# A decoder block on one core: k's copy on ScalarE's queue, two places for q and k, reciprocals turned in squares, later fetches

## The chip, the cores and the metric

The kernel runs on one of the eight cores of a Trainium2 chip. The metric is the device time of one execution in microseconds (us); lower is better. A core has five engines that run their own lists of instructions and wait for each other by semaphores: TensorE (PE, matrix products; its weight loads are shown as PEld), VectorE (DVE), ScalarE (ACT), GpSimd (POOL) and SyncE (SP, which here only issues DMA transfers). Transfers are carried out by 16 DMA engines.

## The reference

One layer of a decoder block on x of 512 tokens by 1024 channels, in float32:

```
h = rmsnorm(x);  z = h @ w_in, split into q_r, k_r, v_r, g_r, q_f, k_f, v_f, f_f, a_r, a_f
y_r = W_ro(silu(g_r) * GroupNorm(retention(rot(q_r), rot(k_r), v_r)))      4 heads
y_f = W_fo(attention(norm(q_f), norm(k_f), v_f, log_f))                    8 heads of 64
x = x + W_out(sigmoid(a_r) * y_r + sigmoid(a_f) * y_f)
x = x + W_down(silu(h2 @ W_gate) * (h2 @ W_up)),  h2 = rmsnorm(x)
```

The change lies in the attention of y_f. With c the running sum of log_f, per head:

```
s[q, k] = q.k / 8 + c[q] - c[k]   for k <= q, else -inf
o[q] = sum_k exp(s[q,k] - max) v[k] / sum_k exp(s[q,k] - max)
```

## The kernel before, in words

Channels or tokens lie on the 128 partitions of SBUF. Each matrix product in float32 is made of three products of rounded parts (high and low), written as `three(...)`. Weights come in tiles of 128x1024 (512 KB, raw), are split by ACT (`wh`, line 164) and DVE (`wl`, line 165), and are used by PE. PE's list of instructions is pinned: it runs in the order in which the program names the products (`in_order`, line 65). So does SP's list from line 831 on: `move` (line 71) chains all its transfers, and a transfer that must wait for another holds back all that stand behind it.

The attention runs over 8 heads in four pairs a (heads e = 0 and 1 of a pair lie on the lower and upper 64 partitions), and over four blocks i of 128 queries. The loop at line 914 takes one step s for each (a, e, i), 32 steps, and then some more; n = s % 8 is the step within a pair. In each step stand, in this order:

- `fox_prep` (line 692): scales k (part 0) or q (part 1) of a head. ACT writes the high part to its 64 partitions of tile `tk` or `tq`, DVE writes the low part (for k into `kl`, whose other half is zero). For k, `fox_twice` (line 703) has SP copy the high part to the other 64 partitions by a transfer tk<-tk.
- `fox_scores` (line 713): two products of q with k on PE into one of four PSUM banks; GpSimd adds the mask to the bias `cb`; DVE adds the bias and takes the minimum (line 730); ACT takes the exponential with the row sums (line 732) into `pr`, `rs`.
- `fox_turn` (line 735), two steps later: DVE turns `pr` within squares of 32x32 into `psq` (line 744).
- `fox_put` (line 746): SP stores the squares to DRAM (pd<-psq, 640 KB) and, after the second head of a pair, DVE takes the reciprocals of the row sums `ri` (line 752) and SP stores them turned, as rd<-ri.
- `fox_get` (line 756): SP fetches the squares in turned order (pT<-pd, four transfers of 160 KB) and, for the second head, each reciprocal row spread over 64 partitions (rw<-rd).
- `fox_values` (line 766): 16 products of v with pT, then DVE scales by `rw` (line 776), and ACT and DVE split the result into `ofh`, `ofl`.

Between these, `fill(us)` puts products that do not depend on attention (the projection's last groups, the gates, then the retention branch's output) into PE's list until they fill so many microseconds: `SF` = 0.63, 0.83, 1.57, 1.4 for i = 0 to 3, `VF` = 1.8 ahead of the products with v, `TAIL` = 2.6 in the steps after the last scores. The order of PE's list does not depend on when anything arrives.

For pair a, scores stand at n = 0 to 7. q and k of head 1 are prepared at n = 0 and 1 of the same pair, those of the next pair's head 0 at n = 4 and 5. Squares are put at n = 7 (head 0) and at n = 3 of the next pair (head 1); fetched two steps after that; and the products with v of pair a stand at n = 0 two pairs later. `tk`, `tq` and `kl` have one place for each head of a pair; `pT` has two places.

Of the kernel before, what the change touches and what calls it, by code (L numbers as in the profile page):

```python
# [9 lines left out]
F32 = mybir.dt.float32  # L10
F32R = mybir.dt.float32r
# [3 lines left out]
ALU = mybir.AluOpType  # L15
AX = mybir.AxisListType

P = 128
D = 1024
S = 512  # L20
NT = S // P
NK = D // P
RH, RDK, RDV = 4, 64, 128
FH, FD = 8, 64
# [3 lines left out]
MM3 = 3 / 2400.0  # L28
WARM = 8 * (512,) + 3 * (128,)
NEG = -1e30  # L30
PAD_CST, PAD_FTOK, PAD_SM = 104, 104, 32

C_GMIX = 0
C_GFFN = C_GMIX + NK
# [19 lines left out]
def block_kernel(ctx: ExitStack, tc, x, xT, c_early, c_tab, c_late, w_qf, w_tok, w_vg, w_a, w_y, w_o, w_gu, w_gl, w_dn, w_dh, out):  # L54
    nc = tc.nc
    PS = bass.MemoryType.PSUM
    tt, ts, stt = nc.vector.tensor_tensor, nc.vector.tensor_scalar, nc.vector.scalar_tensor_tensor
# [3 lines left out]
    def after(ins, prev):  # L61

        tc.add_manual_dep(ins.ins, prev.ins.name, mybir.DependencyInfo(mybir.DependencyClass.NoSync, mybir.DependencyReason.DATA), reason="order")
# [7 lines left out]
    def move(to, src):  # L71

        ins = nc.sync.dma_start(out=to, in_=src)  # L73
        if moves[0]:
            if moves[1] is not None:
                after(ins, moves[1])
            moves[1] = ins
        return ins
# [3 lines left out]
    def mm(o, **kw):  # L82
        in_order(nc.tensor.matmul(o, **kw))  # L83
# [4 lines left out]
    def f32(ap):  # L88
        return ap.bitcast(F32)
# [5 lines left out]
    drp = tc.alloc_tile_pool(name="drp", bufs=1, space=bass.MemoryType.DRAM)  # L95
    rwk = tc.alloc_tile_pool(name="rwk", bufs=2, side="left")
    sm = ctx.enter_context(tc.tile_pool(name="sm", bufs=2, side="right"))
# [104 lines left out]
    for k in range(NK):  # L202
# [11 lines left out]
        first = nc.vector.tensor_copy(out=h[:, cs], in_=raw)  # L214
# [7 lines left out]
    for k in range(NK):  # L222
        h, l = first_units[k // 2]
# [29 lines left out]
    nc.gpsimd.memset(ones, 1.0)  # L253
    nc.gpsimd.tensor_scalar_mul(gq, ce[:, C_GQ:C_GQ + 1], FD ** -0.5)
    gk = ce[:, C_GK:C_GK + 1]

    def broadcast_cols(r, dst, wide=None, behind=None):

# [259 lines left out]
    gp = nc.gpsimd  # L518
    ret = [{} for _ in range(NT)]
    fox = {}  # L520
# [137 lines left out]
    def fox_bias(h):  # L658

        cb = fwk.tile([P, S], F32, name="cb", tag="cb", bufs=CBUF)  # L660
        move(cb, cd[h:h + 1, :].broadcast_to([P, S]))
        return cb

    ra, rb = slice(0, FD), slice(FD, P)
# [27 lines left out]
    def fox_prep(a, e, part):  # L692

        r, o = ((ra, rb), (rb, ra))[e]
        z, g = ((kf, gk), (qf, gq))[part]
        zr, gr = z[r, a, :], g[r]
        h = fwk.tile([P, S], F32R, name=("tk", "tq")[part], tag=f"{('tk', 'tq')[part]}{e}", bufs=1)
        act(out=h[r], in_=zr, func=AF.Copy, scale=gr)
        to = h[o] if part else kls[e][r]
        stt(out=to, in0=zr, scalar=gr, in1=f32(h)[r], op0=ALU.mult, op1=ALU.subtract)  # L700
        fox[("k", "q")[part], e] = h

    def fox_twice(e):

        r, o = ((ra, rb), (rb, ra))[e]
        move(f32(fox["k", e])[o], f32(fox["k", e])[r])

    def next_bank():

        fox["banks"] = fox.get("banks", 0) + 1  # L710
        return bank(("sc", "tp")[fox["banks"] % 2])

    def fox_scores(a, e, i):

        tq, tk, kl = fox["q", e], fox["k", e], kls[e]
        if i == NT - 1:
            fox["cb"] = fox["bias"].pop(0)
            if e == 0:
                fox["rs", a] = sm.tile([P, 2, NT], F32, name="rs", tag="rs", bufs=2)
        cb = fox["cb"]  # L720
        n = (i + 1) * P
        m = max(n, 256)
        qs = slice(i * P, n)
        gp.tensor_tensor(out=cb[:, qs], in0=cb[:, qs], in1=mask, op=ALU.add)
        sc = next_bank()
        mm(sc[:, :m], lhsT=tq[:, qs], rhs=tk[:, :m], start=True, stop=False)
        mm(sc[:, :m], lhsT=tq[:, qs], rhs=kl[:, :m], start=False, stop=True)
        pr = fwk.tile([P, n], F32, name="pr", tag=f"pr{i}", bufs=1)
        nm = sm.tile([P, 1], F32, name="nm", tag="nm", bufs=4)
        nc.vector.tensor_tensor_reduce(out=pr[:, :n], in0=cb[:, :n], in1=sc[:, :n], scale=-1.0, scalar=3e38,  # L730
                                       op0=ALU.add, op1=ALU.min, accum_out=nm)
        fox["last"] = act(out=pr[:, :n], in_=pr[:, :n], func=AF.Exp, scale=-1.0, bias=nm, accum_out=fox["rs", a][:, e, i:i + 1])  # L732
        fox["pr", a, e, i] = pr
# [12 lines left out]
    def fox_put(a, e):  # L746

        pd = fox["pd", e] = drp.tile([4, 32, 4, 320], F32, name="pd", tag=f"pd{e}")
        move(pd.rearrange("g m b x -> (g m) (b x)"), fox["sq", a, e].rearrange("p b c j -> p (b c j)"))
        if e:  # L750
            ri = sm.tile([P, 2, NT], F32, name="ri", tag="ri", bufs=2)
            nc.vector.reciprocal(out=ri, in_=fox["rs", a])
            rd = fox["rd", e] = drp.tile([2, NT, P], F32, name="rd", tag="rd")
            move(rd.rearrange("e i p -> p e i"), ri)

    def fox_get(a, e):

        pT = fox["pT", a, e] = fwk.tile([P, 4, 320], F32, name="pT", tag="pT", bufs=PT)
        for b in range(4):
            move(pT[32 * b:32 * b + 32], fox["pd", e][:, :, b, :].rearrange("g m x -> m g x"))  # L760
        if e:
            rw = fox["rw", a] = fwk.tile([P, S], F32, name="rw", tag="rw", bufs=1)
            for h, rows in enumerate((ra, rb)):
                move(rw[rows], fox["rd", e][h:h + 1].rearrange("o i p -> o (i p)").broadcast_to([FD, S]))

    def fox_values(a):

        av = next_bank()
        o = av.rearrange("p (g i j) -> p g i j", g=4, i=NT)
        for k in range(NT):  # L770
            c = TRI[k] + k
            for e in range(2):
                mm(o[e * FD:(e + 1) * FD, :, k:, :].rearrange("p g i j -> p g (i j)"), lhsT=vf[:, k, (2 * a + e) * FD:(2 * a + e + 1) * FD],
                   rhs=fox["pT", a, e][:, :, 32 * c:32 * (c + NT - k)], start=k == 0, stop=k == NT - 1)
        o = o.rearrange("p g i j -> p i g j")
        first = tt(out=o, in0=o, in1=fox["rw", a].rearrange("p (i g j) -> p i g j", i=NT, g=4), op=ALU.mult)
        after(first, split_raw.last[1])
        if a == 3:
            after(first, y_ret.last)
        h, l = (f[:, a, :].rearrange("p (i g j) -> p i g j", i=NT, g=4) for f in (ofh, ofl))  # L780
        cast = nc.scalar.copy(out=h, in_=o)
        after(cast, split_raw.last[0])
        if a == 3:
            after(cast, sigmoid.last)
        tt(out=l, in0=o, in1=f32(h), op=ALU.subtract)
# [110 lines left out]

    fwk = tc.alloc_tile_pool(name="fwk", bufs=2, side="left")
    ofp = tc.alloc_tile_pool(name="ofp", bufs=1, side="right")
    kls = [fwk.tile([P, S], F32R, name="kl", tag=f"kl{e}", bufs=1) for e in range(2)]
    for e, o in enumerate((rb, ra)):  # L900
        gp.memset(f32(kls[e])[o], 0.0)

    fill(CF[2])
    fox["bias"] = [fox_bias(0)]
    for part in range(2):
        fox_prep(0, 0, part)
    fill(CF[3])
    fox_twice(0)
    fox["bias"].append(fox_bias(1))
    fill(PF)  # L910
    ofh = ofp.tile([P, 4, S], F32R, name="ofh")
    ofl = ofp.tile([P, 4, S], F32R, name="ofl")
    chain = [(a, e, i) for a in range(4) for e in range(2) for i in reversed(range(NT))]
    for s in range(len(chain) + 9):
        a, n = s // 8, s % 8
        if n < 2 and a < 4:
            fox_prep(a, 1, n)
        if n in (4, 5) and a < 3:
            fox_prep(a + 1, 0, n - 4)
        if s < len(chain):  # L920
            fox_scores(*chain[s])
        if n == 1 and a < 4:
            fox_twice(1)
        if n == 5 and a < 3:
            fox_twice(0)
        if n in (1, 5) and 2 * a + n // 4 + 2 < FH:
            fox["bias"].append(fox_bias(2 * a + n // 4 + 2))
        if n == 0 and a > 1:
            fill(VF)
            if a == 2:  # L930
                fill.until(8)
            if a == 5:
                ready.append(split_raw(begun.pop(0)))
            fox_values(a - 2)
        if n == 7 and a < 4 or n == 3 and 0 < a < 5:
            fox_put(*chain[s - 7 + 3][:2])
        if n in (1, 5) and 0 < a < 5:
            fox_get(*chain[s - 9 + 3][:2])
        if LAG <= s < len(chain) + LAG:
            fox_turn(*chain[s - LAG])  # L940
        fill(SF[chain[s][2]] if s < len(chain) else TAIL)
# [336 lines left out]
    for k in range(HALF + 2, NF):  # L1278
        prepare(k)
        if k - HALF - 2 in (0, 2):  # L1280

            half = (k - HALF - 2) // 2
            name = ("xfh", "xfl")[half]
# [3 lines left out]
        if k - HALF - 2 in (0, 4):  # L1287
            half = (k - HALF - 2) // 4
            put_squares(SQUARES[-1], half)
            name = ("xfh", "xfl")[half]  # L1290
# [84 lines left out]
    for g in range(4):  # L1375
        if g < 3:
            ws.append(factors(w_dh[g + 1]))
        o = pf[:, g % 2, HALF + 4 * (g // 2):HALF + 4 * (g // 2) + 4, :]
        rows = [out[m * P:(m + 1) * P, :] for m in (2 * g, 2 * g + 1)]
# [7 lines left out]
        x, y, z = (bank(t)[:, 0:HT] for t in ("sc", "acc", "acc"))  # L1387
# [134 lines left out]
```

## Time and profile before

| what | value |
|---|---|
| median of 3 runs | 713.64 us (712.75 to 715.49) |
| profiled execution, its own time | 712.57 us |
| its span, first to last instruction | 710.8 us |
| mean granted clock of TensorE | 0.988 |
| PE, DVE, ACT, POOL busy | 689.8, 534.4, 352.9, 70.1 us |
| moved by DMA | 98.30 MB, 95887 packets |
| attention's first scores to its last products with v | 187.3 to 300.4 us |

How to read it: the profile is one execution. A line of a timeline gives start, duration, engine, line of the kernel, operation and operands, and in brackets the idle time just before and what ended it. In "tk<-tk" the left name is what is written. A row of waits gives who waited for whom: total, times, longest. A stretch's row gives the busy time of each engine in it, the granted clock of TensorE as a share of full speed, the busy share of the DMA engines, and what they moved in GB/s. A transfer's row gives its size and the microseconds from issue to landing. SPq is SP issuing.

### The profile page before, as it was taken

Reading aid. Unit: us, or ns where it says so; the run is one execution under the profiler, and the core shown is the slowest. Engines: PE = TensorE matmul, PEld = TensorE weight load, DVE = VectorE, ACT = ScalarE, POOL = GpSimd, SP = SyncE. Lnnn points to the kernel's source line nnn. Section 1 sums busy time; section 2 is a strip of 40 time slices with the busy share of each in tenths; the row PEclk is TensorE's granted clock in tenths of the full one; section 3 lists DMA queues with packets and bytes.
Section 4 is the critical chain, followed back from the end, with each engine's and each line's share of the span. In section 5 each row is a group of like instructions: output and inputs, shape, how many; then the busy total and the mean of one; then the engine's idle time right before and its main releaser. Section 6 shows DMA issues by size and latency. Waiting matters only on the chain.

```text
span 710.8 us, 9375 instructions
## 1 busy us (share of the span) xinstructions
PE 689.8 (97%) x3407; PEld 568.8 (80%) x3407; DVE 534.4 (75%) x857; ACT 352.9 (50%) x518; POOL 70.1 (10%) x88
## 2 busy tenths in 40 slices
PE   8999999999987888999999999999999999999998
PEld 5888988888774566788887888888888898888898
DVE  6898488765595662378799898888989889556784
ACT  6767453233462443254557656464656466334251
POOL 0004940200221210000031000000000000000000
PEclk9999999999998998999999999999999999999999
DMA  8900315437478798433921333637271441551221
GB/s 293 414 8 30 120 60 146 114 105 174 154 187 200 171 192 222 148 118 101 325 109 60 134 116 89 200 86 206 48 214 35 119 161 42 142 190 60 72 96 71
DMA packets 95887, 98.30 MB, mean 138 GB/s; under 512 B 67928, under 2 KB 72664, under 8 KB 95328
## 3 DMA queue, kind: packets, MB, share of 16 engines
q1 hardware_dynamic: 95696, 97.67, 46.9%
q8 instruction: 27, 0.44, 0.3%
q14 instruction: 20, 0.16, 0.1%
q10 hardware_dynamic: 144, 0.02, 0.0%
HBM read 81.90 MB, written 9.47 MB: 129 GB/s over the span
## 4 chain that ended last, share of the span: by engine, by line
PE 85%; DMA 9%; DVE 3%; issue 1%; SPq 1%; ACT 1%; DVEq 0%; ACTq 0%
PE acc L83 65%; PE sc L83 14%; PE tp L83 5%; DMA pd<-psq 4%; DMA pT<-pd 3%; DMA raw<-in_w_tok_dram 1%; SPq L73 1%; PE tp L86 1%; DMA raw<-in_w_a_dram 1%; DVE pr L730 0%; DVE wl L165 0%; ACT ps L1042 0%; DVE psq L744 0%; DVE ps L1043 0%; DVE b L1051 0%
## 5 line engine op out<-in xcount | busy, mean ns | idle before, releaser
L83 PE MATMUL acc<-ps,xfh 128*128 128x512 f32 (+1 forms) x576 | 167.7, 373 | 0.4 <-ACT us L1164 0.4
L83 PEld LDWEIGHTS acc<-ps,xfh 128*128 128x128 f32 x576 | 105.1, 188 | 20.3 <-ACT us L1164 0.6
L1042 ACT CAST ps<-b 128x1024 fp32r<-128x1024 f32 (+1 forms) x84 | 82.3, 980 | 60.9 <-PE acc L83 26.2
L1043 DVE TENSOR_TENSOR ps<-b,ps 128x1024 fp32r<-128x1024 f32 (+1 forms) x84 | 94.4, 1135 | 22.2 <-ACT ps L1042 21.0
L83 PE MATMUL acc<-ps,xfl 128*128 128x512 f32 (+1 forms) x288 | 107.5, 373 | 0.0
L164 ACT CAST wh<-raw 128x1024 fp32r<-128x1024 f32 (+1 forms) x44 | 46.1, 1049 | 90.5 <-PE acc L83 42.9
L165 DVE TENSOR_TENSOR wl<-raw,wh 128x1024 fp32r<-128x1024 f32 (+1 forms) x44 | 55.3, 1259 | 17.6 <-ACT wh L164 17.6
L83 PEld LDWEIGHTS acc<-ps,xfl 128*128 128x128 f32 x288 | 54.2, 188 | 10.4 <-DVE xfl L1005 0.5
L83 PE MATMUL acc<-xh,wh 128*128 128x512 f32 x128 | 52.5, 410 | 0.0
L83 PE MATMUL acc<-xh,wl 128*128 128x512 f32 x128 | 51.7, 404 | 0.8 <-DVE wl L165 0.8
L1051 DVE TENSOR_TENSOR b<-b,b 128x1024 f32<-128x1024 f32 (+1 forms) x48 | 52.1, 1126 | 0.0
L83 PE MATMUL acc<-xl,wh 128*128 128x512 f32 x128 | 51.7, 404 | 0.0
L83 PE MATMUL acc<-wh,xh 128*128 128x512 f32 (+2 forms) x144 | 50.7, 352 | 0.0
L83 PE MATMUL acc<-wh,xl 128*128 128x512 f32 (+2 forms) x144 | 49.8, 346 | 0.0
L83 PE MATMUL acc<-wl,xh 128*128 128x512 f32 (+2 forms) x144 | 49.7, 345 | 0.0
L83 PE MATMUL acc<-hl,ps 128*128 128x512 f32 x168 | 40.8, 392 | 0.0
L83 PEld LDWEIGHTS acc<-hl,ps 128*128 128x128 f32 x168 | 31.6, 188 | 7.0
L1164 ACT COPY us<-acc 128x512 f32<-128x512 f32 (+1 forms) x48 | 26.2, 551 | 17.3 <-PE acc L83 16.3
L732 ACT ACTIVATE pr<-pr,nm 128x512 f32<-128x512 f32 (+3 forms) x32 | 18.0, 561 | 25.8 <-DVE nm L730 25.6
L1083 DVE TENSOR_TENSOR ps<-raw,ps 128x1024 fp32r<-128x1024 f32 x14 | 17.1, 1223 | 17.9 <-ACT ps L1080 17.9
L83 PEld LDWEIGHTS acc<-xh,wl 128*128 128x128 f32 x128 | 24.9, 194 | 7.1 <-DVE wl L165 1.2
L83 PEld LDWEIGHTS acc<-wh,xh 128*128 128x128 f32 x144 | 27.1, 188 | 3.9 <-DVE sT L564 0.2
(301 smaller groups left out, 1458.7 us busy)
## 6 DMA issues: line engine op xcount, KB each, us to landing
b<-in_w_gu_dram SPq DMA_DIRECT2D x40, 512.0 KB, 4.8
raw<-in_w_a_dram SPq DMA_DIRECT2D x16, 512.0 KB, 4.5
raw<-in_w_dn_dram SPq DMA_DIRECT2D x14, 512.0 KB, 4.3
pd<-psq SPq DMA_DIRECT2D x8, 640.0 KB, 6.7
pT<-pd SPq DMA_DIRECT2D x32, 160.0 KB, 4.2
pf<-squares SPq DMA_DIRECT2D x160, 32.0 KB, 1.9
blk<-in_w_vg_dram SPq DMA_DIRECT2D x8, 512.0 KB, 7.7
raw<-in_w_tok_dram SPq DMA_DIRECT2D x8, 512.0 KB, 3.5
```

What stands on the lines that cost most here:

```text
L73: ins = nc.sync.dma_start(out=to, in_=src)
L83: in_order(nc.tensor.matmul(o, **kw))
L86: in_order(nc.tensor.transpose(out=o, in_=src, identity=ident))
L164: split_raw.last = (nc.scalar.copy(out=h[:, :width], in_=raw[:, :width]), tt(out=l[:, :width], in0=raw[:, :width], in1=f32(h)[:, :width], ...
L165: tt(out=l[:, :width], in0=raw[:, :width], in1=f32(h)[:, :width], op=ALU.subtract))
L732: fox["last"] = act(out=pr[:, :n], in_=pr[:, :n], func=AF.Exp, scale=-1.0, bias=nm, accum_out=fox["rs", a][:, e, i:i + 1])
L1042: part.cast = nc.scalar.copy(out=h, in_=raw)
L1043: low = tt(out=l, in0=raw, in1=f32(h), op=ALU.subtract)
L1051: queue(tt(out=raws[g][b][v], in0=raws[g][b][v], in1=raws[g][c][v], op=ALU.add))
L1083: tt(out=l, in0=raw, in1=f32(h), op=ALU.subtract)
L1164: copy = nc.scalar.copy(out=u_(tp, slot), in_=os[tp][:, :w])
```

## The change

Five edits in the attention stage, in one diff:

- k's copy to the other 64 partitions is issued from ACT's list, right behind ACT's scaling, instead of from SP's chained list.
- `tk`, `tq` get two places per head, `kl` two sets by the pair's parity. Preparation moves: head 0 of the next pair at n = 2 and 3, head 1 at n = 6 and 7 (the first pair's head 1 stays at steps 0 and 1).
- The 8 columns of reciprocals go into a zeroed tile of 128x32, DVE turns its four squares of 32x32, and 128 rows of 32 numbers are stored; the fetch takes four pieces of 128 numbers for each partition, and `rw`'s order within a row becomes (g, i, j) instead of (i, g, j).
- `fox_get` stands three steps behind `fox_put` instead of two, and `fox_values` one step later, behind the scores of n = 1; the loop has one step more.
- The pad of the pool of small tiles is 16 columns instead of 32.

```diff
-PAD_CST, PAD_FTOK, PAD_SM = 104, 104, 32
+PAD_CST, PAD_FTOK, PAD_SM = 104, 104, 16
...
+    ri = sm.tile([P, 32], F32, name="ri", tag="ri", bufs=1)
+    nc.gpsimd.memset(ri, 0.0)
...
-        h = fwk.tile([P, S], F32R, name=("tk", "tq")[part], tag=f"{('tk', 'tq')[part]}{e}", bufs=1)
+        h = fwk.tile([P, S], F32R, name=("tk", "tq")[part], tag=f"{('tk', 'tq')[part]}{e}", bufs=2)
         act(out=h[r], in_=zr, func=AF.Copy, scale=gr)
-        to = h[o] if part else kls[e][r]
+        if part == 0:
+            nc.scalar.dma_start(out=f32(h)[o], in_=f32(h)[r])
+        to = h[o] if part else kls[a % 2][e][r]
         stt(out=to, in0=zr, scalar=gr, in1=f32(h)[r], op0=ALU.mult, op1=ALU.subtract)
-        fox[("k", "q")[part], e] = h
-
-    def fox_twice(e):
-
-        r, o = ((ra, rb), (rb, ra))[e]
-        move(f32(fox["k", e])[o], f32(fox["k", e])[r])
+        fox[("k", "q")[part], a, e] = h
...
         if e:
-            ri = sm.tile([P, 2, NT], F32, name="ri", tag="ri", bufs=2)
-            nc.vector.reciprocal(out=ri, in_=fox["rs", a])
-            rd = fox["rd", e] = drp.tile([2, NT, P], F32, name="rd", tag="rd")
-            move(rd.rearrange("e i p -> p e i"), ri)
+            nc.vector.reciprocal(out=ri[:, 0:2 * NT], in_=fox["rs", a].rearrange("p e i -> p (e i)"))
+            rt = sm.tile([P, 32], F32, name="rt", tag="rt", bufs=1)
+            nc.vector.transpose(out=rt, in_=ri)
+            rd = fox["rd", e] = drp.tile([P, 32], F32, name="rd", tag="rd")
+            move(rd, rt)
...
             for h, rows in enumerate((ra, rb)):
-                move(rw[rows], fox["rd", e][h:h + 1].rearrange("o i p -> o (i p)").broadcast_to([FD, S]))
+                row = fox["rd", e].rearrange("(g x) j -> x g j", g=4)[4 * h:4 * h + 4].rearrange("i g j -> g i j")
+                row = bass.AP(tensor=row.tensor, offset=row.offset, ap=[[0, FD], [32 * 32, 4], [1, 4 * 32]])
+                move(rw[rows].rearrange("p (g x) -> p g x", g=4), row)
...
-    kls = [fwk.tile([P, S], F32R, name="kl", tag=f"kl{e}", bufs=1) for e in range(2)]
-    for e, o in enumerate((rb, ra)):
-        gp.memset(f32(kls[e])[o], 0.0)
+    kls = [[fwk.tile([P, S], F32R, name="kl", tag=f"kl{b}{e}", bufs=1) for e in range(2)] for b in range(2)]
+    for pair in kls:
+        for e, o in enumerate((rb, ra)):
+            gp.memset(f32(pair[e])[o], 0.0)
...
-    for s in range(len(chain) + 9):
+    for s in range(len(chain) + 10):
         a, n = s // 8, s % 8
-        if n < 2 and a < 4:
-            fox_prep(a, 1, n)
-        if n in (4, 5) and a < 3:
-            fox_prep(a + 1, 0, n - 4)
+        if n % 4 < 2 and s < 4:
+            fox_prep(0, 1, n)
+        if n % 4 in (2, 3) and a < 3:
+            fox_prep(a + 1, n // 4, n % 4 - 2)
...
-        if n == 0 and a > 1:
+        if n == 1 and a > 1:
             fill(VF)
...
-        if n in (1, 5) and 0 < a < 5:
-            fox_get(*chain[s - 9 + 3][:2])
+        if n in (2, 6) and 0 < a < 5:
+            fox_get(*chain[s - 10 + 3][:2])
```

More of the change, by code (lines that the diff above doesn't have):

```diff
@@ L713, in fox_scores @@
     def fox_scores(a, e, i):
-        tq, tk, kl = fox["q", e], fox["k", e], kls[e]
+        tq, tk, kl = fox["q", a, e], fox["k", a, e], kls[a % 2][e]
         if i == NT - 1:
@@ L775, in fox_values @@
         o = o.rearrange("p g i j -> p i g j")
-        first = tt(out=o, in0=o, in1=fox["rw", a].rearrange("p (i g j) -> p i g j", i=NT, g=4), op=ALU.mult)
+        first = tt(out=o, in0=o, in1=fox["rw", a].rearrange("p (g i j) -> p i g j", i=NT, g=4), op=ALU.mult)
         after(first, split_raw.last[1])
@@ L907, in block_kernel @@
     fill(CF[3])
-    fox_twice(0)
     fox["bias"].append(fox_bias(1))
@@ L913, in block_kernel @@
     chain = [(a, e, i) for a in range(4) for e in range(2) for i in reversed(range(NT))]
-    for s in range(len(chain) + 9):
+    for s in range(len(chain) + 10):
         a, n = s // 8, s % 8
-        if n < 2 and a < 4:
-            fox_prep(a, 1, n)
-        if n in (4, 5) and a < 3:
-            fox_prep(a + 1, 0, n - 4)
+        if n % 4 < 2 and s < 4:
+            fox_prep(0, 1, n)
+        if n % 4 in (2, 3) and a < 3:
+            fox_prep(a + 1, n // 4, n % 4 - 2)
         if s < len(chain):
             fox_scores(*chain[s])
[L922 to L927, printed above, removed]
-        if n == 0 and a > 1:
+            if n in (1, 5) and 2 * a + n // 4 + 2 < FH:
+                fox["bias"].append(fox_bias(2 * a + n // 4 + 2))
+        if n == 1 and a > 1:
             fill(VF)
```

## The prediction

> **What bounds the kernel now.** I read the page's busy times first, then the chain of waits of TensorE (PE), then the stretches that those waits name, then the transfers in them.
>
> ```profile
> PE 689.8 (97%) x3407; PEld 568.8 (80%) x3407; DVE 534.4 (75%) x857; ACT 352.9 (50%) x518; POOL 70.1 (10%) x88
> ```
>
> PE is busy for 97% of the span, so an edit that touches no matrix product can win only what PE waits, and what it runs slowly. PE's own waits are nearly all of one place:
>
> ```profile
> PE tp L83 <- DMA tk<-tk: 6.8, 1, 6.8
> PE tp L83 <- DMA pT<-pd: 4.1, 1, 4.1
> PE sc L83 <- DMA tk<-tk: 3.1, 1, 3.1
> ```
>
> Two are for k's copy (tk), one for the turned exponentials (pT); all lie in the attention steps. The stretches, with columns span, PE, PEld, DVE, ACT and POOL busy, granted clock, DMA share, GB/s:
>
> ```profile
> 211.40:218.25 6.85, 0.02 (x1) 0.03 (x1) 5.09 (x14) 2.65 (x8) 0.46 (x1) 0.83 0.83 14
> 218.25:222.70 4.45, 4.45 (x11) 3.48 (x11) 1.36 (x3) 0.81 (x2) 0.87 (x2) 0.50 0.96 218
> 238.75:241.90 3.15, 0.06 (x1) 0.03 (x1) 1.89 (x5) 2.40 (x6) 0.32 (x1) 1.00 0.11 11
> 243.25:246.60 3.35, 3.35 (x8) 1.76 (x7) 2.37 (x7) 0.82 (x2) 0.46 (x1) 0.50 1.07 247
> 264.60:268.70 4.10, 0.00 (x0) 0.02 (x1) 1.26 (x2) 1.04 (x1) 0.00 (x0) 0.80 0.89 229
> 268.70:273.90 5.20, 5.19 (x16) 2.96 (x17) 0.66 (x1) 0.00 (x0) 0.00 (x0) 0.50 0.54 209
> 208.00:218.00 10.00, 3.42 (x17) 2.69 (x16) 8.43 (x22) 4.40 (x11) 1.38 (x3) 0.89 0.68 23
> 235.00:243.00 8.00, 4.91 (x24) 3.79 (x23) 5.90 (x15) 3.97 (x10) 2.31 (x4) 1.00 0.43 43
> 257.00:265.00 8.00, 7.58 (x33) 5.35 (x31) 5.37 (x19) 2.62 (x8) 1.39 (x3) 1.00 0.91 59
> ```
>
> Rows 1, 3 and 5 are the idle stretches; behind each, rows 2, 4 and 6, PE runs at half clock. The last three rows tell why: from 208 to 218 us the DMA engines are busy for 0.68 of the time and move 23 GB/s. Something occupies them and carries nothing. What the queue of SP issued there, and what that stretch's transfers took:
>
> ```profile
> 207.28 0.38 SPq L73 DMA_DIRECT2D rd<-ri  x1
> 207.76 0.54 SPq L73 DMA_DIRECT2D tk<-tk  x1
> 208.39 0.54 SPq L73 DMA_DIRECT2D cb<-cd  x1
> 210.25 3.69 SPq L73 DMA_DIRECT2D pT<-pd  x4
> ```
>
> ```profile
> DMA packets 1250, 0.59 MB, mean 53 GB/s; under 512 B 1072, under 2 KB 1072, under 8 KB 1250
> ...
> tk<-tk SPq DMA_DIRECT2D x1, 128.0 KB, 10.4
> ```
>
> And how long the four transfers of the reciprocals took to land:
>
> ```profile
> DMA to landing us min/median/max: 10.6/11.9/11.9
> ```
>
> The reciprocals, 4 KB, go out as `rd.rearrange("e i p -> p e i")`: 1024 single elements, which are the 1072 small packets. The first takes 10.6 us, and tk, issued 0.5 us later on the same queue, lands 10.4 us after its issue, when PE has stood since 211.4. The other two waits have an rd ahead of them as well (the last two rows of the stretches). So the culprit is the form of a 4 KB transfer, and the waits on tk and pT are its symptoms.
>
> **The change part by part.** First what there is to win, in the profiled execution (712.57 us, span 710.8; the runs' median is 713.64, so 1.07 us above it).
> Idle: 6.85 + 3.15 + 4.10 = 14.1 us.
> Half clock: half of 4.45 + 3.35 + 5.20 = 13.0, so 6.5 us.
> Waits inside the products with v:
>
> ```profile
> 223.02 1.07 PE L83 MATMUL sc<-pT,vf 128*64 128x512 f32 x2
> 224.38 2.34 PE L83 MATMUL sc<-pT,vf 128*64 128x512 f32 x14 [0.29 <-DMA pT<-pd]
> ...
> 245.75 3.64 PE L83 MATMUL tp<-pT,vf 128*64 128x512 f32 x16
> ...
> 298.08 2.38 PE L83 MATMUL sc<-pT,vf 128*64 128x512 f32 x16
> ```
>
> The last 16 products run unhindered in 2.4; the first set takes 3.7 (to 226.72), the second 3.6, of which 0.4 is clock already counted; the third's first two took about 0.8 too long. Together 1.3 + 0.8 + 0.8 = 2.9. In all 23.5 us; it is gone only if all three edits below work.
>
> *The reciprocals in squares.* Gone: 1024 elements of 4 B. New: 128 rows of 128 B, one DVE transpose of 128x32, and a fetch whose rows are four pieces of 512 B in place of one of 2 KB. Prices from the nearest rows:
>
> ```profile
> pd<-psq SPq DMA_DIRECT2D x8, 640.0 KB, 6.7
> pT<-pd SPq DMA_DIRECT2D x32, 160.0 KB, 4.2
> ...
> kf<-zd SPq DMA_DIRECT2D x4, 256.0 KB, 5.6
> ```
>
> kf<-zd writes runs of 128 B, 2048 a transfer, in 5.6 us; a sixteenth of that many cannot take longer, so rd lies between nearly nothing and 5.6; I take 3, nearer the small end. The fetch gets 512 pieces instead of 128 a pair, a quarter of one kf's and four times as long each: inside 5.6 as well, and needed only when the products are done. The transpose is under the 282 ns below, four times, 1.1 us of DVE at most:
>
> ```profile
> L744 DVE STREAM_TRANSPOSE psq<-pr 128x128 f32<-128x128 f32 x16 | 4.5, 282 | 0.0
> ```
>
> *k's copy on ScalarE, two places.* The copy leaves SP's list, where it stood behind rd and behind SP's waits for pd, and is prepared six steps ahead of its first product instead of three to four:
>
> ```profile
> 187.20:211.40 24.20, 24.20 (x115) 20.03 (x113) 21.68 (x59) 15.59 (x37) 7.27 (x14) 1.00 0.67 201
> 199.60:211.40 11.80, 11.80 (x56) 9.69 (x54) 11.07 (x31) 7.47 (x19) 2.73 (x6) 1.00 0.77 216
> 187.20:275.00 87.80, 73.45 (x313) 54.83 (x312) 58.27 (x151) 38.24 (x88) 16.99 (x30) 0.90 0.80 192
> 153.00:172.00 19.00, 19.00 (x92) 15.53 (x91) 11.07 (x32) 4.98 (x6) 1.04 (x2) 1.00 0.61 148
> ```
>
> ```profile
> L73 SPq DMA_DIRECT2D tk<-tk x8: 467/485/692, 176.0 to 245.6; - x8
> ```
>
> Eight steps take 11.8 us, so six give 8.9. A landing behind rd took 10.4; without rd, a fifth of what the four pT move (four at 160 KB against one of 128) should not take longer than pT's 4.2. ACT pays eight issues of about 0.5 us (SP's price), 4 us over the whole stage, and is busy 7.47 of 11.80: hidden. A new wait: the issue waits for the scaled copy just ahead on ACT, and the next exponentials queue behind it; half a microsecond, against three steps (4.4 us) that PE's four score banks allow. The two further memsets go to POOL, whose only work from 153 to 172 us is the old two (1.04): hidden. DVE is close to full, 11.07 of 11.80; the work is the same but moves forward. DVE spent 21.7 + 5.1 us from 187.2 to 218.25 (5.1 is in the first idle stretch) on what PE will now pass in 24.2, so it falls some 2.6 us behind, inside the same 4.4 us. I charge nothing, up to 2.6.
>
> *Fetches a step later.* The products with v move with them. From putting the squares (n = 3) to using them there were five steps and 1.8 us of filling, 9.2 us; now six, 10.7. Needed are the landings of pd and of pT, 6.7 + 4.2 = 10.9, as measured with rd in the way. So this is what is late next: by the medians 0.2 us at each of three places, none if both get faster, and several if the engines are crowded. I take 2.5 us in all, bounds 0 and 14.5 (rival 1). At the end the last products come one step (2.6 us) later, with other filling ahead of them:
>
> ```profile
> 300.39 0.50 PE L83 MATMUL acc<-orh,wh 128*128 128x512 f32 x1
> 308.19 0.39 PE L83 MATMUL acc<-ofh,wh 128*128 128x512 f32 x1
> ```
>
> Between the last products with v and the first use of ofh lie 7.8 us; 5.2 remain, hidden still. The pad of the small tiles moves no work: nothing.
>
> Sum: 712.57 - 23.5 + 2.5 = 691.6; plus the 1.07 between profile and median, 692.6: I say 692.5.
>
> **The rivals.**
> *1. The DMA engines become the bound* (27%). Of the 87.8 us from 187.2 to 275 they were busy 0.80, 70 us. rd's part is 6.8 + 3.4 + 7.3 = 17.5 us in its three stretches, less about 3.7 for the 1.05 MB that moved beside it (at 216 / 0.77 = 280 GB/s): 13.8. So 56 us of transfers must pass in 64 to 66 us, 85 to 88%. Against it: in the first 24.2 us PE ran without a wait at a share of 0.67. If each of two or three fetches comes 3.15 us late and costs half clock as the second wait did (3.35 / 2), that is 4.8 each: 698.7 to 703.6 (two or three), about a microsecond more in the median. The Trainium skill, "DMA: Bandwidth & Descriptors", section "Issuing engines are not separate DMA queues", speaks for this rival: transfers issued from ScalarE run on the same 16 engines as those from SP, and the second issuer saves only sequencer time. By that rule the copy's new queue wins nothing by itself, and the gain hangs on rd alone; no run here shows it yet. On the clock its "TensorE: Matmul & The Clock Gate", section "What's actually happening", lets the clock fall after an idle window of about 3.4 us; by that a 3.15 us wait could be free, and this rival would end near 697 to 699. The row differs: 3.15 us idle was followed by 0.50.
>
> *2. The transfer stays slow* (8%): a landing of rd near 10 us whatever its form, with tk and pT held up as now; then only the extra step helps, 709 to 714. Against it: kf<-zd moves 16 times as many such rows in 5.6.
>
> *3. Slower: ACT stands at its own queue* (5%). If the issue on ACT holds it until the copy gets through, the exponentials behind it come late, then squares, pd and pT. At 10.4 us a copy, less the 4.4 of slack, six copies inside the chain cost 36 us: 712.6 - 23.5 + 36 = 725. It decides from 4.4 + 23.5 / 6 = 8.3 us a copy on. SP's four issues at 210.25 took 3.69, 0.9 each, with the queues at their fullest: far from 8.3.
>
> **How the numbers follow.** Forecast 60%: 690 to 696. Rival 1 27%: 697 to 705. Rival 2 8%, rival 3 5%. The range reaches from 688 (every microsecond of the 23.5 won gives 690.1 in the median; two below that for the waits I did not count) to 704, leaving out the end of rival 1 and the other two. A measurement of this kernel tells 0.5%, 3.6 us, from no change: faster 0.60 + 0.27 + 0.01 of rival 2 = 0.88, same 0.07, slower 0.05.
>
> **What would show it.** Right: rd's landing under 6 us and no stretch with busy DMA engines at 20 to 60 GB/s; PE's waits on tk gone; the granted clock at 1.00 through the steps; the products with v at 2.4 us; what is left of waiting named pT. Wrong: rd still near 10 us (rival 2); waits on pT of 3 us or more at a high DMA share (rival 1); ACT idle behind its own issues and PE waiting for score banks (rival 3); or PE waiting for DVE, which would mean that the 2.6 us are not covered.

## The result, and the profile after

The changed kernel takes 684.48 us (median of four executions), the kernel before 713.32 us on the same chip: a ratio of 0.9585 [0.9557, 0.9613], or 28.8 us. The forecast was 692.5 us with a range of 688 to 704, so the direction is right and the size is not: the time lies 8 us below the forecast and 3.5 us below the lower end. Three of the four took 683.42 to 684.76 us, and the ratio is theirs; the fourth ran at a granted clock of 0.851 throughout (743 us). The profile shown is of the repeat described below (685.45 us, span 683.7).

The head of the page after, with the granted clock in 40 slices:

```profile
span 683.7 us, 9374 instructions
...
PE 676.1 (99%) x3407; PEld 566.4 (83%) x3407; DVE 534.3 (78%) x861; ACT 354.7 (52%) x518; POOL 70.0 (10%) x91
...
PEclk9999999999999999999999999999999999999999
```

The same row of the page before:

```profile
PEclk9999999999998998999999999999999999999999
```

PE's idle time is 683.7 - 676.1 = 7.6 us; before it was 710.8 - 689.8 = 21.0. So 13.4 us of the 27.1 between the two spans come from idle time, and 13.7 from products that are busy for less time. The slices at reduced clock are gone, and that is part of the 13.7. It can't be all: the forecast counted 6.5 us for it, and 2.9 for waits inside the products with v.

PE's waits after (in total, times, longest):

```profile
PE acc L83 <- DVE wl L165: 1.5, 1, 1.5
PE tp L83 <- DVE warm L114: 1.2, 1, 1.2
PE sc L83 <- DVE wh L214: 0.8, 1, 0.8
PE tp L83 <- DMA pT<-pd: 0.4, 1, 0.4
PE acc L83 <- ACT us L1162: 0.3, 1, 0.3
PE sc L83 <- DMA pT<-pd: 0.3, 1, 0.3
```

The two waits for k's copy are gone, and of the 4.4 us for pT (4.1 and 0.3) 0.7 are left, in two places. The transfers of the attention stage after, first by group (KB each, median us to landing), from 184 to 282 us:

```profile
pd<-psq SPq DMA_DIRECT2D x8, 640.0 KB, 5.5
pT<-pd SPq DMA_DIRECT2D x32, 160.0 KB, 4.1
...
tk<-tk ACTq DMA_DIRECT2D x4, 128.0 KB, 4.0
rd<-rt SPq DMA_DIRECT2D x4, 16.0 KB, 4.8
```

The reciprocals land in 4.8 us (median; 4.3 to 7.9) where they took 11.9, k's copy in 4.0 where the one behind them took 10.4. The issues of k's copy on ACT, for all eight:

```profile
L702 ACTq DMA_DIRECT2D tk<-tk x8: 468/476/519, 173.3 to 213.7; - x8
```

And the attention stage by windows, from the first scores to the first use of ofh (span, PE, PEld, DVE, ACT and POOL busy, granted clock, DMA share, GB/s), with its two most crowded stretches below; then the same stage before:

```profile
186.40:284.70 98.30, 97.66 (x459) 76.37 (x458) 68.12 (x167) 50.11 (x103) 15.54 (x30) 1.00 0.73 220
212.00:232.00 20.00, 19.64 (x93) 15.02 (x92) 15.42 (x45) 10.18 (x25) 5.08 (x10) 1.00 0.93 253
232.00:256.00 24.00, 23.72 (x115) 17.16 (x114) 17.70 (x48) 10.16 (x22) 2.77 (x6) 1.00 0.81 261
```

```profile
187.30:308.20 120.90, 106.55 (x460) 80.60 (x459) 71.76 (x167) 52.05 (x107) 16.99 (x30) 0.93 0.75 182
```

The stage went from 120.9 to 98.3 us. Those 22.6 us are a little more than the forecast had for the whole change (23.5 - 2.5 = 21.0). The rest, 27.1 - 22.6 = 4.5 us of span, lies outside the attention, in stages whose instructions the change does not touch. The same 32 products with ofh, before and after (ns min/median/max, first and last start):

```profile
L83 PE MATMUL acc<-ofh,wh x32: 392/395/398, 308.2 to 329.9; 128*128 128x512 f32 x32
```

```profile
L83 PE MATMUL acc<-ofh,wh x32: 389/389/389, 284.7 to 305.8; 128*128 128x512 f32 x32
```

From the first to the last they take 21.7 us before and 21.1 after. Between the first and the last of the 32 lie 31 groups of three, 93 steps: 0.2333 us a product before, 0.2269 after, 2.7% less, without a wait on either side. The duration of one (395 and 389 ns) shows the difference weakly, since products overlap; the spacing is what counts. Products of this shape are in every stage. That is the part of the 28.8 us that the forecast did not have.

### The profile page after: what moved, and what is told of

It is laid out like the page before. It is cut to its first block, busy times and chain, and to the rows that moved or that the text cites. A ratio compares the mean times of both kernels' runs of the same rounds, so it can differ in the third digit from the quotient of the medians.

```text
span 741.4 us, 9374 instructions
## 1 busy us (share of the span) xinstructions
PE 735.5 (99%) x3407; PEld 581.3 (78%) x3407; DVE 538.3 (73%) x861; ACT 354.5 (48%) x518; POOL 70.0 (9%) x91
## 3 DMA queue, kind: packets, MB, share of 16 engines
q10 hardware_dynamic: 784, 1.07, 0.5%
## 4 chain that ended last, share of the span: by engine, by line
PE 73%; DVE 0%; issue 0%
PE acc L83 56%; PE sc L83 12%; PE tp L83 4%; PE tp L86 0%; DVE pf L1407 0%
## 5 line engine op out<-in xcount | busy, mean ns | idle before, releaser
L83 PE MATMUL acc<-ps,xfh 128*128 128x512 f32 (+1 forms) x576 | 180.0, 396 | 0.0
L83 PEld LDWEIGHTS acc<-ps,xfh 128*128 128x128 f32 x576 | 108.1, 194 | 28.3
L83 PE MATMUL acc<-ps,xfl 128*128 128x512 f32 (+1 forms) x288 | 114.1, 396 | 0.0
L83 PEld LDWEIGHTS acc<-ps,xfl 128*128 128x128 f32 x288 | 55.7, 193 | 13.7
L83 PE MATMUL acc<-xh,wl 128*128 128x512 f32 x128 | 53.4, 417 | 1.4 <-DVE wl L165 1.4
L83 PE MATMUL acc<-xl,wh 128*128 128x512 f32 x128 | 53.3, 417 | 0.0
L83 PE MATMUL acc<-wh,xh 128*128 128x512 f32 (+2 forms) x144 | 53.2, 369 | 0.0
L83 PE MATMUL acc<-wh,xl 128*128 128x512 f32 (+2 forms) x144 | 52.1, 362 | 0.0
L83 PE MATMUL acc<-wl,xh 128*128 128x512 f32 (+2 forms) x144 | 52.0, 362 | 0.0
L83 PE MATMUL acc<-hl,ps 128*128 128x512 f32 x168 | 44.4, 417 | 0.0
L83 PEld LDWEIGHTS acc<-wh,xl 128*128 128x128 f32 x144 | 28.0, 194 | 4.7
```

## The experiments

The change has three parts of work, called squares (the reciprocals turned in squares), k's copy (on ScalarE, two places, earlier preparation) and later fetch. It also moves addresses. The tiles at the right-hand end of SBUF are laid down from the top, the small tiles first: before, ri has 2 x 32 bytes a partition and the pad 128, together 192; after, ri 128, rt 128 and the pad 64, together 320. Everything below them starts 128 bytes lower. In the built programs xh starts at byte 194176 of its partition before, which is 128 past a multiple of 256, and at 194048 after, a multiple of 256.

My theory after the result: the squares carry the gain of the attention stage, as forecast, and the start addresses of product operands carry the rest. The rival: the products run faster for another reason that comes with the work (a clock that never falls, quieter transfers), and the pad does nothing. The runs stand in three groups, each on one chip with its own runs of the kernel before (714.04 us for the first four, 714.33 for the next four, 714.86 for the last four). A ratio is always to the kernel before in the same group; a difference of less than a microsecond between groups shows nothing.

**The changed kernel once more.** No edit.

> The changed kernel once more, for an undisturbed profile. Expected 683 to 686 us. The sum had 23.5 us to win and the runs show 28.8. Theory A (the waits were counted too small): PE idle falls by about 15 us and the rest lies between 187 and 300 us of the old span, the stage as a whole being 28 us shorter. Theory B (something outside the stage): the stage is 23 us shorter and about 5 us are missing after it, with equal counts of products.

684.75 us (683.69 to 685.75), ratio 0.9583 [0.9553, 0.9612]. The result stands, and theory B came true: the stage is 22.6 us shorter, and 4.5 us are missing outside it. The profile is the one shown above.

**The squares alone.** The two other parts undone, the pad of the changed kernel left:

```
-        if part == 0:
-            nc.scalar.dma_start(out=f32(h)[o], in_=f32(h)[r])
+    def fox_twice(e):
...
+        move(f32(fox["k", e])[o], f32(fox["k", e])[r])
...
-        if n in (2, 6) and 0 < a < 5:
-            fox_get(*chain[s - 10 + 3][:2])
+        if n in (1, 5) and 0 < a < 5:
+            fox_get(*chain[s - 9 + 3][:2])
```

> Only the reciprocals in squares; k's copy, one place and old fetch steps as before. Theory 1 (rd's 1024 elements hold up everything behind them): 690 to 697 us, rd lands in under 6 us, no stretch with busy DMA engines at under 60 GB/s, tk's waits gone or under 1 us, pT's 0 to 2 us each. Theory 2 (tk's place in SP's list and its short lead are the cause): 707 or more, tk's waits stay.

686.91 us (686.76 to 687.34), ratio 0.9614 [0.9587, 0.9641]: all but 2.2 us of the change, and below the 690 to 697 that were expected, because these addresses are the new ones too (the same part at the old ones is timed below). PE's waits in its profile:

```profile
PE sc L83 <- DMA pT<-pd: 1.3, 1, 1.3
...
PE tp L83 <- DMA pT<-pd: 0.8, 1, 0.8
PE tp L83 <- DMA tk<-tk: 0.2, 1, 0.2
```

k's copy is issued by SP and prepared as late as before, and the wait for it falls from 9.9 us to 0.2 (0.6 at the old addresses). So the wait named tk was indeed a symptom of what stood ahead of tk on the queue.

**k's copy alone.** The squares and the later fetch undone:

```
-            nc.vector.transpose(out=rt, in_=ri)
-            move(rd, rt)
+            move(rd.rearrange("e i p -> p e i"), ri)
...
-        if n in (2, 6) and 0 < a < 5:
+        if n in (1, 5) and 0 < a < 5:
```

> Only k's copy on ScalarE's queue, with the two places and the earlier preparation; rd in single elements and old fetch steps. Theory 1: tk's waits go, but rd still lands after 10 us and pT behind it, so the first products with v wait 6 to 9 us in place of the scores: 702 to 711 us. Theory 2: 693 to 698, with pT's waits no longer than before (4.4 us in all).

712.7 us (711.24 to 716.29), ratio 0.9982 [0.9961, 1.0002]: no change, where theory 1 had expected a gain of 3 us or more. PE's waits, and the landing of k's copy:

```profile
PE tp L83 <- DMA pT<-pd: 8.0, 2, 4.5
PE sc L83 <- DMA pT<-pd: 7.1, 1, 7.1
```

```profile
DMA to landing us min/median/max: 2.2/3.8/10.7
```

The waits for tk are gone and 15.1 us for pT stand in their place (before: 4.1 for pT, 14.0 with tk). One copy still took 10.7 us although it had ScalarE's queue to itself. It was issued at 207.98 us, while the reciprocals, issued at 204.72, were under way, and from 208 to 216 us all transfers together moved 13 to 36 GB/s. So SP's list isn't what slowed it; that it shares the DMA engines with the single elements is the reading that fits, and is not shown apart. Here the Trainium skill, "DMA: Bandwidth & Descriptors", section "Issuing engines are not separate DMA queues", agrees with the trace: it says that another issuer saves only the sequencer's time, and this run gives the ratio 0.9982.

**k's copy and later fetch, without the squares.** Only the squares undone. The pad is 32 here, so that without the tiles of the squares xh starts at 194176 again, as in the kernel before:

```
-            rd = fox["rd", e] = drp.tile([P, 32], F32, name="rd", tag="rd")
-            move(rd, rt)
+            rd = fox["rd", e] = drp.tile([2, NT, P], F32, name="rd", tag="rd")
+            move(rd.rearrange("e i p -> p e i"), ri)
```

> The changed kernel with rd in single elements again (copy on ScalarE, two places, later fetches kept). Theory 1: 700 to 710 us, waits on pT or rw behind rd at three places. Theory 2: 684 to 690, the squares add little.

709.88 us (708.56 to 710.09, and once 1740.37), ratio 0.9931 [0.9897, 0.9966]. PE's waits:

```profile
PE tp L83 <- DMA pT<-pd: 8.3, 2, 8.1
PE sc L83 <- DMA pT<-pd: 3.1, 1, 3.1
```

Against k's copy alone the extra step takes about 4 us off the waits for pT, and no more: the slow transfer of the reciprocals still stands ahead of the fetch (issued at 206.45 us, the fetch at 216.18).

**The addresses alone, on the kernel before.** No part of the change; the pad puts xh at 194048, as after:

```
-PAD_CST, PAD_FTOK, PAD_SM = 104, 104, 32
+PAD_CST, PAD_FTOK, PAD_SM = 104, 104, 64
```

> The kernel before with one number changed: the pad of the small tiles is 64 columns instead of 32, so that xh, xl, orh, ofh and the feed-forward's tiles start 128 bytes lower, at the addresses they have in the changed kernel (multiples of 256 bytes). Theory B1 (PE reads operands at these addresses faster): 707.5 to 709.5 us, products of 128x512 at 389 ns outside the attention steps instead of 392 to 395. Theory A (all of the 28.8 us lies in the attention's waits): 712.5 to 715.

707.58 us (705.95 to 708.56), ratio 0.9906 [0.9875, 0.9936]. The products with ofh, and PE's waits:

```profile
L83 PE MATMUL acc<-ofh,wh x32: 389/389/389, 307.0 to 328.1; 128*128 128x512 f32 x32
```

```profile
PE tp L83 <- DMA tk<-tk: 9.8, 1, 9.8
PE sc L83 <- DMA tk<-tk: 4.6, 1, 4.6
PE tp L83 <- DMA pT<-pd: 3.5, 1, 3.5
```

The same instructions with the same waits become faster by 6.7 us, and the products with ofh take 21.1 us again. The rival is out: no part of the work is in this run. PE's waits for transfers grew, from 14.0 to 17.9 us in these rows: where a transfer sets the pace, faster products arrive earlier and wait.

**The change without the move of addresses.** The pad puts xh at 193920, 128 past a multiple of 256, as before:

```
-PAD_CST, PAD_FTOK, PAD_SM = 104, 104, 16
+PAD_CST, PAD_FTOK, PAD_SM = 104, 104, 48
```

> The changed kernel with a pad of 48 columns: the same tiles start at 128 bytes past a multiple of 256, as in the kernel before. Theory B1: 688.5 to 691, products at 392 to 395 ns. Theory A: 684 to 685.5.

691.38 us (691.27 to 691.6), ratio 0.9687 [0.9653, 0.972]. This is the change as the prediction costed it, without the move of addresses, and it is 1.1 us from its 692.5. The products with ofh, and the attention stage between the same two places as above:

```profile
L83 PE MATMUL acc<-ofh,wh x32: 390/392/404, 287.3 to 308.9; 128*128 128x512 f32 x32
```

```profile
187.20:287.30 100.10, 99.20 (x460) 76.54 (x459) 68.77 (x167) 49.76 (x104) 15.53 (x30) 1.00 0.72 216
```

The spacing is the old one (21.6 us), and the stage takes 100.1 us: 20.8 less than before.

**Two more addresses.** The pad at 32 (xh at 193984, 192 past a multiple of 256) and at 80 (193792, a multiple of 256 that is not one of 512):

```
+PAD_CST, PAD_FTOK, PAD_SM = 104, 104, 32
```

> The changed kernel with a pad of 32 columns: the tiles start at 192 bytes past a multiple of 256 (64 past a multiple of 128). If what counts is a multiple of 256: as slow as with 48 columns or slower, 689 to 693. If only multiples of 128 were good and 256 better: slower than with 48. Theory A: 684 to 685.5.

```
+PAD_CST, PAD_FTOK, PAD_SM = 104, 104, 80
```

> The changed kernel with a pad of 80 columns: the tiles start at a multiple of 256 again, 256 bytes lower (256 past a multiple of 512). If a multiple of 256 is what counts: 684 to 685.5 as the changed kernel. If 512 is needed: 688 or more.

At 192 past: 690.35 us (689.87 to 691.53), ratio 0.9675 [0.9634, 0.9716], the slow time. At a multiple of 256: 684.68 us (683.9 to 684.83), ratio 0.959 [0.9557, 0.9623], the fast time. A multiple of 512 isn't needed.

**The squares alone, at the old addresses.** The second experiment with the pad at 48 (xh at 193920):

```
-PAD_CST, PAD_FTOK, PAD_SM = 104, 104, 16
+PAD_CST, PAD_FTOK, PAD_SM = 104, 104, 48
```

In the next texts e2 is the squares alone at the new addresses, and e6 the change with the pad at 48.

> Only the reciprocals in squares, and a pad of 48 columns, so that the tiles start at 128 past a multiple of 256 as in the kernel before. This is the squares' own part. From e2 (686.9) plus the 6.7 us between e6 and the changed kernel: 692 to 695 us, a ratio near 0.972. If the address counts only together with the other edits: 687 to 689.

694.15 us (693.56 to 695.17), ratio 0.9709 [0.9695, 0.9724]. This one part is worth 20.7 us of the 28.8 by itself, against about 7 for the address and 2 to 3 for all the rest.

**The squares with one of the other two parts each.** First with k's copy (the later fetch undone), then with the later fetch (k's copy undone), both at the new addresses:

```
-        if n in (2, 6) and 0 < a < 5:
-            fox_get(*chain[s - 10 + 3][:2])
+        if n in (1, 5) and 0 < a < 5:
+            fox_get(*chain[s - 9 + 3][:2])
```

> The changed kernel without the later fetches (squares, k's copy on ScalarE and two places, new addresses). Of the 2.2 us between e2 and the changed kernel: if they are tk's and the SP list's relief, 684.5 to 685.5 here; if they are the later fetch's, 686.5 to 687.5, with waits on pT of about 2 us.

```
-            nc.scalar.dma_start(out=f32(h)[o], in_=f32(h)[r])
+        move(f32(fox["k", e])[o], f32(fox["k", e])[r])
```

> The changed kernel without k's copy on ScalarE and its two places (squares, later fetches, new addresses). If the later fetch brings what is left: 684 to 685.5, waits on pT under 1 us; if the copy does: 686.5 to 687.5, with waits on tk or pT.

With k's copy: 690.96 us (689.48 to 691.87), ratio 0.9656 [0.9638, 0.9675]. With the later fetch: 687.97 us (687.6 to 688.85), ratio 0.9623 [0.9609, 0.9637]. Both are slower than everything that was expected. The squares alone have 686.91 us, ratio 0.9614, in another group. By the ratios k's copy makes them about 3 us slower (4 by the medians), the later fetch alone changes nothing clear of the noise, and the two together make them 2.2 us faster. PE's waits with k's copy:

```profile
PE tp L83 <- DMA pT<-pd: 3.3, 2, 2.0
...
PE tp L83 <- DVE nm L729: 0.9, 1, 0.9
...
PE sc L83 <- DVE nm L729: 0.5, 1, 0.5
```

The last two are new: PE waits for a score bank that DVE has not read. But DVE is not short of time. Behind those waits stand these of DVE (200 to 260 us) and of POOL (same stretch):

```profile
DVE pr L729 <- POOL cb L723: 7.8, 7, 3.9
```

```profile
POOL cb L723 <- DMA cb<-cd: 7.1, 2, 4.6
```

And SP's list in that place:

```profile
213.08 0.55 SPq L73 DMA_DIRECT2D raw<-in_w_a_dram  x1
219.18 0.35 SPq L73 DMA_DIRECT2D pd<-psq  x1
219.64 0.39 SPq L73 DMA_DIRECT2D raw<-in_w_a_dram  x1
220.12 0.89 SPq L73 DMA_DIRECT2D cb<-cd  x1
```

SP issues nothing from 213.63 to 219.18, and the table of biases (cb), which POOL, DVE and then PE need, stands behind. In the changed kernel cb is issued at 217.27. So the chain is SP's list, cb, POOL, DVE, PE. The profile puts 5.5 us of SP's wait down to the landing of a copy of k; why the earlier fetch sets it off was not tried apart, nor whether the queue or the earlier preparation costs the 3 to 4 us.

With the later fetch alone, one wait for a transfer is left, and the clock shows what it costs (the products with v around it, then the stretch behind it and a longer one):

```profile
212.75 1.07 PE L83 MATMUL tp<-pT,vf 128*64 128x512 f32 x2
216.77 3.94 PE L83 MATMUL tp<-pT,vf 128*64 128x512 f32 x14 [2.95 <-DMA pT<-pd]
```

```profile
217.00:220.00 3.00, 3.00 (x11) 1.59 (x10) 1.73 (x3) 1.46 (x3) 0.15 (x1) 0.50 0.81 250
212.00:232.00 20.00, 17.05 (x74) 12.29 (x73) 15.87 (x41) 10.47 (x26) 4.36 (x9) 0.91 0.88 247
```

After 2.95 us of idle the 14 products take 3.94 us instead of 2.34, at a granted clock of 0.50. The Trainium skill, "TensorE: Matmul & The Clock Gate", section "What's actually happening", gives an idle window of about 3.4 us before the clock falls; the idle times recorded here (2.95 us, and 3.15 before the change) are shorter. How far they contradict it is open, since the ends of products are modelled in these profiles: the two products ahead of this wait are recorded with 1.07 us, where sixteen unhindered ones take 2.38. The longest wait in the run with k's copy, 2.0 us, cost no clock (granted 1.00).

**The other operand.** The changed kernel, its right-hand tiles at the fast address, with the tiles at the left-hand end of SBUF moved by 128 bytes: wh and wl start 128 past a multiple of 256 (byte 14464 in place of 14336).

```
-PAD_CST, PAD_FTOK, PAD_SM = 104, 104, 16
+PAD_CST, PAD_FTOK, PAD_SM = 136, 104, 16
```

> The changed kernel with the pad of the other side's constants 32 columns larger: the weight tiles wh, wl, raw and qf, kf, vf start at 128 past a multiple of 256, while xh, xl, orh, ofh stay on multiples of 256. If the address of either operand of a product counts: 688 to 692, products at 392 ns or more where a weight tile is read; if only the first-named side counted: 684 to 685.5.

691.21 us (691.07 to 694.17), ratio 0.9676 [0.9655, 0.9698]: the slow time again.

```profile
L83 PE MATMUL acc<-ofh,wh x32: 390/393/405, 287.0 to 308.6; 128*128 128x512 f32 x32
```

So it is not only the operand that the change moved: with the tiles of the other end off by 128 the whole is lost again (6.5 us here, 6.7 with the right-hand tiles off). But the same trace shows products that stay fast. In this kernel mgh starts at 42112, so that mgh and the weight tiles both start 128 past a multiple of 256:

```profile
L83 PE MATMUL acc<-mgh,wh x64: 388/390/393, 309.3 to 352.1; 128*128 128x512 f32 x64
```

From the first to the last of these lie 63 groups of three, 189 steps in 42.8 us: 0.2265 us a product. The kernel before, in which mgh and the weight tiles both start at a multiple of 256, takes the same 42.8 us (its row is shown in the next section). So a start off a multiple of 256 does not cost by itself; products are slow where their two operands start at different places within 256 bytes:

| kernel | product | first and second operand, bytes past a multiple of 256 | us a product |
|---|---|---|---|
| changed | ofh, wh | 0, 0 | 0.2269 |
| before | ofh, wh | 128, 0 | 0.2333 |
| changed, pad 48 | ofh, wh | 128, 0 | 0.2323 |
| changed, left-hand tiles moved | ofh, wh | 0, 128 | 0.2323 |
| before | mgh, wh | 0, 0 | 0.2265 |
| changed, left-hand tiles moved | mgh, wh | 128, 128 | 0.2265 |

## Why the prediction was wrong, step by step

**The step that failed** is a sentence of the sum: "The pad of the small tiles moves no work: nothing." It moves no work, but with the two new tiles it moves addresses, and they were worth 691.38 - 684.68 = 6.7 us. The same assumption opens the prediction, where an edit that touches no matrix product can win only what PE waits and what it runs slowly: the products outside the attention were not taken to run slowly, and part of them did (those with ofh at 0.2333 us each, where 0.2269 is possible). Nothing in the prediction chose the 16 columns for their address, so that the tiles landed at a fast one was luck: with the pad of 32 columns as before, the same change takes 690.35 us, inside the range. Without the addresses the forecast holds (691.38 against 692.5), with them the time falls out of the range, whose lower end allowed 2 us beyond every counted microsecond. Nothing in the profile of before named this cost. But the rows were there to ask about: the products with ofh at 392/395/398 and those with mgh at 389 have the same shape, engine and clock, and differ by nothing that the prediction had accounted for:

```profile
L83 PE MATMUL acc<-mgh,wh x64: 389/389/395, 330.6 to 373.4; 128*128 128x512 f32 x64
```

In the built program mgh starts at 41984, a multiple of 256 as the weight tiles do, and ofh at 128640, 128 past one.

**The culprit** was right. "The culprit is the form of a 4 KB transfer, and the waits on tk and pT are its symptoms": the squares alone take the tk waits from 9.9 to 0.2 us, and k's copy alone wins nothing.

**The gain of the stage** came to 20.8 us at the old addresses, against 21.0, but by two errors that cancel. Idle there fell from 120.90 - 106.55 = 14.35 to 0.90 us: the forecast took off 14.1 and gave back 2.5, where only 0.9 came back. Busy time fell by 106.55 - 99.20 = 7.35 us, where 6.5 + 2.9 = 9.4 was forecast. The 2.9 for waits inside the products with v were not all to be had, because the first two of a set still start ahead of their data, as the changed kernel's row shows:

```profile
214.41 1.07 PE L83 MATMUL tp<-pT,vf 128*64 128x512 f32 x2
215.84 2.34 PE L83 MATMUL tp<-pT,vf 128*64 128x512 f32 x14 [0.36 <-DMA pT<-pd]
```

That set takes 3.8 us from its start to its end, and the first one before took 3.7; "the products with v at 2.4 us" came true for two of the four sets.

**The new form of the reciprocals** was priced at 3 us with a bound of 5.6. The median is 4.8, inside the bound and nearer its large end; the slowest of the four took 7.9, so the bound, and the sign "rd's landing under 6 us", failed once. No wait of PE came of it. The transposes are 4 at 186 ns, 0.7 us against a bound of 1.1.

**The issues on ACT** take 0.476 us against "about 0.5", and PE waits nowhere for ACT in the stage. Rival 3 (ACT stands at its queue) is out, and not only because the copy got faster: with the copy alone one took 10.7 us to land, and the longest issue was still under 0.6.

**DVE's 2.6 us** were covered, as forecast: PE has no wait for a score bank after. Without the later fetch such waits do come (1.4 us), but by way of SP's list and POOL, and not because DVE is full.

**Rival 1** (the DMA engines as the bound) did not come true. It worked out a share of 85 to 88% over 64 to 66 us; over such a stretch the changed kernel has 0.80:

```profile
186.40:251.00 64.60, 63.96 (x301) 50.57 (x299) 53.97 (x150) 35.14 (x82) 15.54 (x30) 1.00 0.80 238
```

In the most crowded part of it, 212 to 232 us, the share was 0.93 and PE's wait 0.36 us. With the squares and the later fetch alone a share of 0.88 in the same place goes with a wait of 2.95 us, so the share by itself does not decide; what does was not tried apart. **Rival 2** is out: the reciprocals land in 4.3 to 7.9 us.

**The three edits are not a sum.** The forecast said that the 23.5 us are "gone only if all three edits below work". In fact one of them brings 20.7 us, and the other two matter only as a pair: k's copy is worth about 3 us with the later fetch (684.75 against 687.97) and costs 3 to 4 without it.

## What to carry to other kernels

A wait is named after the transfer that is late, and the cause can stand ahead of it in the same queue: look for a stretch in which the DMA engines are busy and carry little, and mend that transfer before moving the others to another queue. A changed tile size is a changed address for every tile laid down after it: before a change is costed, and before a gain is put down to its work, compare the durations of products of one shape across their operands, look up where each product's two operands start, and time the kernel with the old addresses restored. Test the parts alone and in pairs: here one part carried nearly all, and a second was a loss until a third came with it.

## What the runs showed of the hardware

The rate of float32 products depends on how the starts of their two operands in SBUF lie to each other. In five of the runs above the work is the same and only starts move: 684.68 and 684.75 us where all the large tiles start at a multiple of 256 bytes; 691.38, 690.35 and 691.21 us where those of one end of SBUF start 128 or 192 bytes past one. Product by product, the table above puts the loss where the two starts differ within 256 bytes (0.2323 to 0.2333 us a product of 128x512), and none where both are 0 or both 128 past (0.2265 to 0.2269). Why is not shown: no view tells what a product reads when. Differences other than 128, 192 and multiples of 256 bytes, and types other than float32, were not looked at.

Single elements of 4 bytes are dear out of proportion to their bytes: 1024 of them (4 KB) took 10.6 to 12.8 us in the four kernels' traces that have them, where 128 rows of 128 bytes (16 KB) took 4.8 in the median. With k's copy alone, one copy on another engine's queue took 10.7 us beside them, against a median of 3.8.

No version that was run beats the changed kernel: pad 80 has 684.68 us where it has 684.75.
